# One PSUM pool for attention and the last layer, and a fixed order for TensorE's steps in a two-layer decoder trunk

## The chip, the cores and the metric

The kernel runs on one core of a Trainium2 chip. The metric is the time of one execution in microseconds (us) on the device; where several runs are compared, their median. The engines are called as in the profile: PE is TensorE (matmuls; PEld its weight loads), DVE is VectorE, ACT is ScalarE, POOL is GpSimd, SP is SyncE, which here issues DMAs. PSUM is the buffer that matmuls write to. It has eight banks, of 128 partitions by 512 fp32 numbers each.

## The reference, cut to what matters

512 tokens of width 1024, with 16 learned meta tokens ahead of them (528 positions), go through two layers and a final norm:

```python
h = concatenate([meta, x])                               # 528 x 1024
for i in range(2):
    a = rmsnorm(h, norm_mix[i])
    h = h + (pool_mixer(a, ...) if i == 0 else sb_mixer(a, w_qkv, w_o))
    n = rmsnorm(h, norm_ffn[i])
    h = h + (silu(n @ w_gate[i]) * (n @ w_up[i])) @ w_down[i]      # 1024 -> 2816 -> 1024
return rmsnorm(h, final_norm)[16:]

def sb_mixer(h, w_qkv, w_o):                             # 16 heads of 64
    q, k, v = (h @ w_qkv) split into heads
    z = q k^T / 8                                        # mask: key < query
    log_keep = where(mask, log_sigmoid(-z), 0)
    later = reverse_cumsum(log_keep) - log_keep
    a = where(mask, exp(log_sigmoid(z) + later), 0)
    return (a @ v) @ w_o
```

All of it is fp32.

## The kernel before

**Products.** Each fp32 product is made of three products of halves: weight and activation are split into a high part (a cast by ACT) and a low part (a subtraction by DVE), and `mm3` (L104) issues high x high, high x low and low x high into one PSUM tile. `wsplit` (L84) makes the halves of a weight block of 128 x 512; its raw block comes by DMA from SP's queue. In names, `...h` and `...l` are the halves.

**Stages.** Layer 0's pool mixer and feed-forward network (FFN) take the first 402 us, stick-breaking attention runs to about 685 us, layer 1's FFN and the final norm to the end.

**Attention** goes over eight pairs of heads. `proj` (L512) projects q, k and v of a pair in five steps of eight `mm3` each, into tiles `pj`; the first of all, `pj0_00`, is followed by the norm's product `abp` (ones x sums of squares, `norm_bcast` L167), whose result scales every projection. `Scores.group` (L572) makes the scores z of both heads in three groups, 832, 0 and 416, with a sigmoid of z (`sg`) and of -z (`kp`) by ACT behind each. DVE then runs, head by head, a reverse scan over `kp` (L594) and a product with `sg` (L596). `turned` (L603) transposes `sg` on PE (tiles `t1`, `t2`; `am` is a small strip that ACT copies for the last transpose), ACT and DVE split the result (`a1..`, `a2..`, and four small `a0` steps), and `attend` multiplies it with v into `po`. `wo` gives steps of the output projection, `pw{p0}_{c}`: product of the pairs from p0 on, added to the residual chunk `h{c}` by DVE (L673). The main loop interleaves: while pair p's weights are made, PE works on the projections of pair p+2, or, when none are left, on `wo` steps: w[0:4] (`pw2_0` to `pw2_3`) between pairs 6 and 7, w[4:6] behind the first transposes of pair 7.

**FFN of layer 1.** 22 blocks of 128 hidden columns. Blocks 0 to 3 are plain (`plain` L356: gate and up, tiles `pp`, operands `f1uh`, `f1ul`); inside block 0's up product the norm's product `fb1p` is made, from which DVE builds the scale `fb1` and, under `operands`, the normalized operands of the other blocks. Blocks 4 to 21 use Strassen's scheme (`strassen` L405): seven products instead of eight, in three PSUM accumulators pa, pb and pc: product 0 and 3 in pa, 1, 4 and 6 in pb, 2 and 5 in pc. The halves `m1`, `m6`, `m5` and `m67` are copied out by ACT (`keep`, L425) before the next product is accumulated onto pa, pb, pc and pb. Six ROUNDS of blocks each end in a down projection by tokens (`down_n` L323, tiles `pd`): 128 tokens x 512 columns (e = 0 or 1), added to `hn` by DVE. A round's down products are spread among the blocks of the next round. The last round's come at the end, by tokens t, each followed by `square` and `store` of `final` (L739): sums of squares by ACT, the root, a scale by ACT for the first 512 columns and by DVE for the other 512, two DMAs.

**PSUM.** Each stage opens a pool of its own (`phase` L66, `ps` L71): `ps1` with six tiles "w" and two "d" for layer 0's FFN, `ps2` with four "one" and two "two" (two banks each) for attention, `ps3` again with six "w" and two "d" for layer 1's FFN. A new pool's tiles wait until the old pool's banks are free.

**Order.** The engines execute their queues in order. A scheduler of the framework sets those orders when the program is built; `tc.issue_after(x)` makes it put what follows behind x. It also tracks, tile by tile, who must wait for whom. `begin` (L679) orders the scores' groups 0 and 1 behind the steps in `before`, and group 2 behind the steps in `between`.

Of the kernel before, what the change touches and what calls it, by code (L numbers as in the profile page):

```python
# [52 lines left out]
def trunk(ctx: ExitStack, tc: tile.TileContext, x, meta, x_t, gain, pool_w, w_qkv, w_o, w_gate, w_up, w_down,  # L53
# [49 lines left out]

    def mm3(outs, wh, wl, xh, xl, start, stop, more=False):  # L104

        for i, (w, xx) in enumerate(((wh, xh), (wh, xl), (wl, xh))):
            for o, sl in outs:
                last = nc.tensor.matmul(o, lhsT=w, rhs=xx[:, sl], start=start and i == 0, stop=stop and i == 2,  # L108
                                        skip_group_check=more)
# [164 lines left out]
    def ffn(layer, gcol, norm, after):  # L274
# [48 lines left out]
        def down_n(r, t, e, hid, w, tag="d", sl=slice(0, 512)):  # L323
# [8 lines left out]
            for j, (wh, wl) in enumerate(zip(*w)):  # L332
                for i, (x_, w_) in enumerate(((0, wh), (1, wh), (0, wl))):
                    nc.tensor.matmul(pd, lhsT=hid[j][x_][:, ts], rhs=w_[:, sl], start=r > 0 and i + j == 0,  # L334
                                     stop=j == len(hid) - 1 and i == 2, skip_group_check=r == 0)
# [3 lines left out]
            else:  # L339
                nc.vector.tensor_tensor(out=hv, in0=pd, in1=hv, op=ALU.add)  # L340
# [473 lines left out]
```

## Time and profile before

| what | value |
|---|---|
| runs | 1045.97, 1046.10, 1046.62 us; median 1046.1 |
| profiled execution | 1047.39 us, its span 1045.6 us, mean granted clock 0.991 |
| PE busy | 1017.1 us, 97% of the span |
| DVE busy | 846.4 us, 81% |
| ACT busy | 550.8 us, 53% |
| DMA | 95.7 MB, 92 GB/s on average |
| last matmul starts | 1037.36 us |

The span is what the profiler saw from the first to the last instruction; the execution's own time is 1.8 us longer. A PE that is busy is not always at its peak, since the ends of matmuls are modelled and the clock can be lower; the view of windows has the granted clock by stretch. In the view of groups and in the timeline a line reads: engine, line, operation, output <- inputs, and in brackets the idle time before it with what ended it. Names there leave out the numbers of layer, pair and buffer, so `pw` is `pw2_1` or any other.

### The profile page before, as it was taken

Reading aid. Unit: us, or ns where it says so; the run is one execution under the profiler, and the core shown is the slowest. Engines: PE = TensorE matmul, PEld = TensorE weight load, DVE = VectorE, ACT = ScalarE, POOL = GpSimd, SP = SyncE. Lnnn points to the kernel's source line nnn. Section 1 sums busy time; section 2 is a strip of 40 time slices with the busy share of each in tenths; the row PEclk is TensorE's granted clock in tenths of the full one; section 3 lists DMA queues with packets and bytes.
Section 4 is the critical chain, followed back from the end, with each engine's and each line's share of the span. In section 5 each row is a group of like instructions: output and inputs, shape, how many; then the busy total and the mean of one; then the engine's idle time right before and its main releaser. Section 6 shows DMA issues by size and latency. Waiting matters only on the chain.

```text
span 1045.6 us, 18479 instructions
## 1 busy us (share of the span) xinstructions
PE 1017.1 (97%) x7278; PEld 943.5 (90%) x7278; DVE 846.4 (81%) x1511; ACT 550.8 (53%) x1115; POOL 6.2 (1%) x16
## 2 busy tenths in 40 slices
PE   8999999999999999999999998999999999999996
PEld 6999999999999998988888886878999999999985
DVE  7999987888787777778888987779888777788755
ACT  7555544445545455455555455555655544445534
POOL 1000000000000010000000000000000000000000
PEclk9999999999999999999999998999999999999998
DMA  9222333333323332211111212122233323233302
GB/s 349 70 83 71 122 101 102 102 100 102 102 82 102 101 122 87 76 41 61 41 51 32 76 46 81 64 89 70 81 112 112 100 90 99 97 114 109 120 23 81
DMA packets 43112, 95.72 MB, mean 92 GB/s; under 512 B 3329, under 2 KB 20097, under 8 KB 43025
## 3 DMA queue, kind: packets, MB, share of 16 engines
q1 hardware_dynamic: 42272, 93.40, 27.2%
q8 instruction: 57, 0.93, 0.4%
q10 hardware_dynamic: 752, 1.14, 0.3%
q14 instruction: 31, 0.25, 0.1%
HBM read 92.43 MB, written 2.10 MB: 90 GB/s over the span
## 4 chain that ended last, share of the span: by engine, by line
PE 84%; DVE 11%; issue 2%; ACT 1%; DMA 1%; SPq 0%; ACTq 0%; DVEq 0%
PE pb L108 15%; PE pd L108 12%; PE pd L334 12%; PE pa L108 10%; PE pc L108 10%; PE pp L108 9%; PE pj L108 9%; DVE kp L594 2%; PE pw L108 2%; PE z L580 2%; DVE a L632 1%; PE t L607 1%; DVE sg L596 1%; PE mix L108 1%; DVE h L673 1%
## 5 line engine op out<-in xcount | busy, mean ns | idle before, releaser
L307 DVE TENSOR_TENSOR h<-pd,h 128x264 f32<-128x264 f32 x96 | 40.9, 427 | 14.9 <-PE pd L108 14.9
L594 DVE TENSOR_TENSOR_SCAN kp<-kp,estrip 128x1344 f32<-128x1344 f32 x16 | 47.3, 2954 | 3.8 <-ACT kp L589 3.4
L94 ACT CAST ws_3h<-rgate 128x512 fp32r<-128x512 f32 x36 | 22.4, 621 | 53.0 <-PE pb L108 47.8
L94 ACT CAST ws_5h<-s 128x512 fp32r<-128x512 f32 x36 | 22.4, 622 | 45.7 <-PE pb L108 33.3
L446 DVE TENSOR_TENSOR u<-pb,m 128x264 f32<-128x264 f32 (+1 forms) x36 | 15.4, 427 | 35.6 <-PE pb L108 35.5
L94 ACT CAST ws_4h<-s 128x512 fp32r<-128x512 f32 x36 | 22.4, 621 | 41.5 <-PE pa L108 24.4
L108 PE MATMUL pa<-xh,ws_0l 128*128 128x264 f32 (+1 forms) x144 | 40.9, 284 | 0.1
L108 PE MATMUL pc<-xh,ws_2h 128*128 128x264 f32 (+1 forms) x144 | 40.7, 282 | 0.3 <-ACT ws_2h L94 0.3
L108 PE MATMUL pa<-xh,ws_0h 128*128 128x264 f32 (+1 forms) x144 | 40.8, 283 | 0.0
L108 PE MATMUL pb<-xh,ws_1h 128*128 128x264 f32 (+1 forms) x144 | 40.8, 283 | 0.0
L108 PE MATMUL pb<-xh,ws_6l 128*128 128x264 f32 (+1 forms) x144 | 40.7, 283 | 0.0
L108 PE MATMUL pc<-xh,ws_2l 128*128 128x264 f32 (+1 forms) x144 | 40.7, 283 | 0.0
L108 PE MATMUL pb<-xl,ws_1h 128*128 128x264 f32 (+1 forms) x144 | 40.7, 283 | 0.0
L108 PE MATMUL pa<-xl,ws_3h 128*128 128x264 f32 (+1 forms) x144 | 40.7, 283 | 0.0
L108 PE MATMUL pb<-xh,ws_4l 128*128 128x264 f32 (+1 forms) x144 | 40.7, 283 | 0.0
L108 PE MATMUL pa<-xh,ws_3h 128*128 128x264 f32 (+1 forms) x144 | 40.7, 283 | 0.0
L108 PE MATMUL pb<-xh,ws_1l 128*128 128x264 f32 (+1 forms) x144 | 40.7, 283 | 0.0
L108 PE MATMUL pb<-xl,ws_4h 128*128 128x264 f32 (+1 forms) x144 | 40.7, 283 | 0.0
L108 PE MATMUL pc<-xl,ws_5h 128*128 128x264 f32 (+1 forms) x144 | 40.7, 282 | 0.0
L108 PE MATMUL pb<-xl,ws_6h 128*128 128x264 f32 (+1 forms) x144 | 40.7, 282 | 0.0
L108 PE MATMUL pc<-xh,ws_5h 128*128 128x264 f32 (+1 forms) x144 | 40.6, 282 | 0.0
L108 PE MATMUL pa<-xl,ws_0h 128*128 128x264 f32 (+1 forms) x144 | 40.6, 282 | 0.0
(1207 smaller groups left out, 4103.9 us busy)
## 6 DMA issues: line engine op xcount, KB each, us to landing
rgate<-in_ffn_w_gate_dram SPq DMA_DIRECT2D x44, 512.0 KB, 3.5
rup<-in_ffn_w_up_dram SPq DMA_DIRECT2D x44, 512.0 KB, 3.5
rd<-in_ffn_w_down_dram SPq DMA_DIRECT2D x42, 512.0 KB, 3.6
rq<-in_sb_w_qkv_dram SPq DMA_DIRECT2D x8, 512.0 KB, 3.4
rk<-in_sb_w_qkv_dram SPq DMA_DIRECT2D x8, 512.0 KB, 3.5
rv<-in_sb_w_qkv_dram SPq DMA_DIRECT2D x8, 512.0 KB, 3.5
rwo<-in_sb_w_o_dram SPq DMA_DIRECT2D x8, 384.0 KB, 3.0
h<-in_x_t_dram SPq DMA_DIRECT2D x8, 264.0 KB, 6.8
```

The costliest lines, as they stand in the source:

```text
L94: nc.scalar.copy(hi, v[:, j:j + w])
L108: last = nc.tensor.matmul(o, lhsT=w, rhs=xx[:, sl], start=start and i == 0, stop=stop and i == 2, skip_group_check=more)
L307: nc.vector.tensor_tensor(out=hv, in0=pd, in1=hv, op=ALU.add)
L334: nc.tensor.matmul(pd, lhsT=hid[j][x_][:, ts], rhs=w_[:, sl], start=r > 0 and i + j == 0, stop=j == len(hid) - 1 and i == 2, skip_group_ch ...
L446: tt(out=u[:, a], in0=pb, in1=m1, op=ALU.add)
L580: nc.tensor.matmul(tz[:, hd, c:c + k1 - k0], lhsT=qq[hs, i * P:(i + 1) * P], rhs=kk[hs, k0:k1], start=j == 0 and c == 0, stop=False, skip_ ...
L594: nc.vector.tensor_tensor_scan(kp[:, hd, ::-1], kp[:, hd, ::-1], estrip[:, ::-1], 1.0, op0=ALU.mult, op1=ALU.max)
L596: return nc.vector.tensor_tensor(out=sg[:, hd, 0:STRIP - 1], in0=sg[:, hd, 0:STRIP - 1], in1=kp[:, hd, 1:STRIP], op=ALU.mult).ins
L607: nc.tensor.transpose(o, sg[:, c0:c0 + n], ident)
L632: nc.vector.scalar_tensor_tensor(a0[r, i], f32(a0h[r]), lo_rows[r], p2[r, 256:384], op0=ALU.mult, op1=ALU.add)
L673: nc.vector.tensor_tensor(out=hT[c][:, TOK], in0=pj, in1=hT[c][:, TOK], op=ALU.add)
```

## The change

Five edits, on one diff:

- **One PSUM pool.** `ps2` now has two tiles "c", two "d" and two "two" (eight banks), and serves attention and layer 1's FFN; `ps3` is gone. "one" takes "c" and "d" in turn. `ps_pair` gives a plain block's two tiles (one two-bank tile, every third time two "c"), `ps_three` a Strassen block's three: pa and pb are the two banks of one tile "two", pc is a "c".
- **The norm's product** `abp` is issued inside the first projection, behind its fifth `mm3` group (k == FB) instead of behind the eighth.
- **`queued`** chains attention's PE steps, so that each is issued behind the one written before it.
- **LATE = 2**: in the last round, the last two down steps of the round before (r = 4, e = 1, t = 2 and 3) are held back and issued behind the last Strassen product (`prods_end`).
- **The last round's down products** are chained token by token; their e = 1 tiles have the tag "c"; the last token's scales and stores are cut into two pieces of 256 columns, with four DMAs instead of two.

```diff
-    def ps(name, tag, banks=1):
+        if tag == "one" and "c" in psum["bufs"]:
+            psum["turn"] = psum.get("turn", 0) + 1
+            tag = "cd"[psum["turn"] % 2]
...
+    def ps_pair(name):
+        if "w" in psum["bufs"]:
+            return [ps(f"{name}{j}", "w") for j in range(2)]
+        psum["pairs"] = psum.get("pairs", 0) + 1
+        if psum["pairs"] % 3 == 0:
+            return [ps(f"{name}{j}", "c") for j in range(2)]
+        pt = ps(name, "two", 2)
+        return [pt[:, 0], pt[:, 1]]
+    def ps_three(name):
+        if "w" in psum["bufs"]:
+            return [ps(f"{name}{j}", "w") for j in range(3)]
+        pt = ps(name, "two", 2)
+        return [pt[:, 0], pt[:, 1], ps(f"{name}c", "c")]
...
-                pa, pb, pc = [ps(f"p{i}{f}", "w")[:, :n] for i in "abc"]
+                pa, pb, pc = [t[:, :n] for t in ps_three(f"p{f}")]
...
                             for t in range(4):
-                                down_n(r - 1, t, e, prev, w)
+                                rest.append(lambda r=r, t=t, e=e, prev=prev, w=w: down_n(r - 1, t, e, prev, w))
+                            while len(rest) > (LATE if r == len(ROUNDS) - 1 else 0):
+                                rest.pop(0)()
...
+            for st in rest:
+                with tc.issue_after(prods_end[0]):
+                    st()
             square, store = after()
...
-                    down_n(r, t, e, prev, ws[e], "dw"[e], sl)
+                    with tc.issue_after(mark) if mark else nullcontext():
+                        mark = down_n(r, t, e, prev, ws[e], "dc"[e], sl)
...
-    with tc.tile_pool(name="att", bufs=1) as ap, phase("ps2", one=4, two=2):
+    ctx.enter_context(phase("ps2", c=2, d=2, two=2))
+    with tc.tile_pool(name="att", bufs=1) as ap:
...
-                if not rbs:
-                    rb = norm_bcast([acc], "ab", "one")
+                    if not rbs and k == FB:
+                        with tc.issue_after(last):
+                            rbs.append(norm_bcast([acc], "ab", "one"))
+                        mark = last_bcast[0]
...
+        pos = []
+        def queue():
+            return tc.issue_after(pos[0]) if pos else nullcontext()
+        def queued(*steps):
+            for st in steps:
+                with queue():
+                    pos[:] = [st()]
...
-            mark = None
-            for st in before:
-                mark = st()
-            with tc.issue_after(mark) if mark else nullcontext():
-                sc.group(0)
-                mark = sc.group(1)
-            for st in between:
-                with tc.issue_after(mark):
-                    mark = st()
-            with tc.issue_after(mark):
-                sc.group(2)
+            queued(*before, lambda: (sc.group(0), sc.group(1))[1], *between, lambda: sc.group(2))
...
+            w = 512 if t < 3 else 256
+            cuts = [slice(o, o + w) for o in range(0, 512, w)]
+            for sl in cuts:
+                nc.scalar.activation(hvs[0][:, sl], box[0][:, 16 + sl.start:16 + sl.stop], AF.Copy, scale=r)
...
-    ctx.enter_context(phase("ps3", w=6, d=2))
     ffn(1, 24, norms[1], final)
```

Three places show how the orders move. The number behind a name's last underscore is only a buffer's.

**PE between pairs 6 and 7.** Rows are PE's; pw2_1 to pw2_3 are `wo` steps, z7_416 the last scores of pair 7. Before:

```order
L108 MATMUL pw2_1_8108<-os4h_7521,wo2_1l0_8105 128x512
L108 MATMUL pw2_2_8146<-os2h_6813,wo2_2h0_8142 128x512
...
L108 MATMUL pw2_2_8146<-os4h_7521,wo2_2l0_8143 128x512
L108 MATMUL pw2_3_8161<-os2h_6813,wo2_3h0_8157 128x512
...
L108 MATMUL pw2_3_8161<-os2h_6813,wo2_3l0_8158 128x512
L580 MATMUL z7_416_8119<-qk7_1h_7770,qk7_0h_7832 128x400 x2
L580 MATMUL z7_416_8119<-qk7_1h_7770,qk7_0h_7832 128x16 x2
...
L586 MATMUL z7_416_8119<-masks_63 128x128
L108 MATMUL pw2_3_8161<-os3h_7141,wo2_3h0_8157 128x512
```

and in the change:

```order
L132 MATMUL pw2_1_8108<-os4h_7521,wo2_1l0_8105 128x512
L625 MATMUL z7_416_8119<-qk7_1h_7770,qk7_0h_7832 128x400 x2
L625 MATMUL z7_416_8119<-qk7_1h_7770,qk7_0h_7832 128x16 x2
...
L631 MATMUL z7_416_8119<-masks_63 128x128
L132 MATMUL pw2_2_8146<-os2h_6813,wo2_2h0_8142 128x512
```

The scores z7_416 move ahead of twelve products: all nine of pw2_2 and the first three of pw2_3. DVE's queue, which works for the same pair, in the change, from the scan of head 0 to the four a0 of head 0:

```order
L639 SCALAR_TENSOR_TENSOR kp7_8056<-kp7_8056,estrip_5463 128x1344
L730 TENSOR_TENSOR h2_68<-pw2_2_8146,h2_68 128x512
L121 TENSOR_TENSOR wo5_2l0_8394<-rwo5_2_8391,wo5_2h0_8393 128x384
L641 TENSOR_TENSOR sg7_8055<-sg7_8055,kp7_8056 128x1343
L639 SCALAR_TENSOR_TENSOR kp7_8056<-kp7_8056,estrip_5463 128x1344
L730 TENSOR_TENSOR h3_69<-pw2_3_8161,h3_69 128x512
L121 TENSOR_TENSOR wo5_3l0_8416<-rwo5_2_8391,wo5_3h0_8415 128x384
L706 TENSOR_TENSOR of6_7905<-po61_8172,sh61_8182 64x512
L641 TENSOR_TENSOR sg7_8055<-sg7_8055,kp7_8056 128x1343
L686 TENSOR_TENSOR a170l_8208<-t170_8194,a170h_8207 128x1024
L686 TENSOR_TENSOR a270l_8210<-t270_8195,a270h_8209 128x256
L689 SCALAR_TENSOR_TENSOR a0_5471<-a0h70_8211,consts_61,t270_8195 32x128 x4
```

Before, h2 and wo5_2l stood ahead of the first scan, h3 and wo5_3l ahead of the first product with sg, and os6l, h4 and wo5_4l ahead of a270l; now h2 stands behind the first scan, h3 behind the second, and the three behind the a0 steps.

**PE at the start of layer 1's FFN.** pw5_6 and pw5_7 are the last `wo` steps, pp0, pp1 and pp20 the gate products of blocks 0, 1 and 2. Before:

```order
L108 MATMUL pw5_5_8465<-os7h_8342,wo5_5l0_8462 128x512
L108 MATMUL pw5_6_8489<-os5h_7901,wo5_6h0_8485 128x512
...
L108 MATMUL pw5_7_8511<-os7h_8342,wo5_7l0_8508 128x512
L108 MATMUL pp0_8574<-f1uh0_8363,wgate0h0_8553 128x512
L108 MATMUL pp0_8574<-f1ul0_8364,wgate0h0_8553 128x512
```

and in the change:

```order
L132 MATMUL pw5_5_8465<-os7h_8342,wo5_5l0_8462 128x512
L132 MATMUL pp0_8570<-f1uh0_8363,wgate0h0_8549 128x512
L132 MATMUL pw5_6_8489<-os5h_7901,wo5_6h0_8485 128x512
...
L132 MATMUL pw5_7_8511<-os7h_8342,wo5_7l0_8508 128x512
L132 MATMUL pp0_8570<-f1ul0_8364,wgate0h0_8549 128x512
L132 MATMUL pp0_8570<-f1uh0_8363,wgate0l0_8550 128x512
L132 MATMUL pp0_8570<-f1uh1_8384,wgate0h0_8549 128x512
L132 MATMUL pp1_8766<-f1uh0_8363,wgate1h0_8745 128x512
L132 MATMUL pp1_8766<-f1ul0_8364,wgate1h0_8745 128x512
```

The first row of pp0 has moved ahead of pw5_6's nine and pw5_7's nine, and the first two of pp1 among pp0's; two of pp20 follow further on, all ahead of fb1p.

**The last Strassen block, 21.** m1, m6, m5 and m67 are the copies of its PSUM halves, ws21 its weights, wd1_18 those of the last down projection. ACT before:

```order
L425 COPY m1_12328<-pa21_12313 128x256
L94 CAST ws21_5h0_12305<-s3_12280 128x512
L94 CAST ws21_6h0_12309<-rup1_21_12275 128x512
L94 CAST wd1_18_0h0_12430<-rd1_18_0_12428 128x512
L94 CAST wd1_18_0h1_12434<-rd1_18_0_12428 128x512
L94 CAST wd1_20_0h0_12440<-rd1_20_0_12438 128x512
L425 COPY m6_12342<-pb21_12314 128x256
L94 CAST wd1_20_0h1_12444<-rd1_20_0_12438 128x512
L425 COPY m5_12356<-pc21_12315 128x256
```

and in the change:

```order
L116 CAST ws21_5h0_12253<-s3_12228 128x512
L116 CAST ws21_6h0_12257<-rup1_21_12223 128x512
L378 CAST hh20_12141<-u20_12132 128x512
L454 COPY m6_12289<-p21_12261 128x256
L454 COPY m5_12303<-p21c_12262 128x256
L116 CAST wd1_18_0h0_12405<-rd1_18_0_12403 128x512
L116 CAST wd1_18_0h1_12409<-rd1_18_0_12403 128x512
L454 COPY m67_12329<-p21_12261 128x256
```

hh20 has moved from ahead of m1 to right ahead of m6, and wd1_18's casts behind m6 and m5. PE in the change at the end of product 1 (ws21_1) and the beginning of product 3 (ws21_3):

```order
L132 MATMUL p21_12261<-xh1_8534,ws21_1h0_12237 128x256
L132 MATMUL p21_12261<-xl1_8541,ws21_1h0_12237 128x256
L132 MATMUL p21_12261<-xh1_8534,ws21_1l0_12238 128x256
L132 MATMUL p21_12261<-xh3_8536,ws21_3h0_12245 128x256
L132 MATMUL p21_12261<-xl3_8543,ws21_3h0_12245 128x256
```

Product 3 follows product 1 at once; before, product 2 lay between them, and a piece of the last down projection between products 3 and 4.

SP's and POOL's queues keep their order; only the last token's two stores have become four.

More of the change, by code (lines that the diff above doesn't have):

```diff
@@ L31 @@
 PLAIN = 4
+LATE = 2
 FB = 4
@@ L102, in wsplit @@
         return his, los
+    last_mm = []
     def mm3(outs, wh, wl, xh, xl, start, stop, more=False):
@@ L109, in mm3 @@
                                         skip_group_check=more)
+        last_mm[:] = [last.ins]
         return last.ins
@@ L333, in down_n @@
                 for i, (x_, w_) in enumerate(((0, wh), (1, wh), (0, wl))):
-                    nc.tensor.matmul(pd, lhsT=hid[j][x_][:, ts], rhs=w_[:, sl], start=r > 0 and i + j == 0,
-                                     stop=j == len(hid) - 1 and i == 2, skip_group_check=r == 0)
+                    last = nc.tensor.matmul(pd, lhsT=hid[j][x_][:, ts], rhs=w_[:, sl], start=r > 0 and i + j == 0,
+                                            stop=j == len(hid) - 1 and i == 2, skip_group_check=r == 0)
             hv = hn[4 * e + t][:, sl]
@@ L340, in down_n @@
                 nc.vector.tensor_tensor(out=hv, in0=pd, in1=hv, op=ALU.add)
+            return last.ins
         with tc.tile_pool(name=f"ffn{layer}", bufs=1) as fp:
@@ L362, in plain @@
                 prods = []
+                pair = None
                 for i, (dst, (wh, wl)) in enumerate(zip((g, u), parts)):
-                    pts = [ps(f"pp{f}", "w")[:, :sl.stop - sl.start] for sl in pieces]
+                    if full or not i:
+                        pair = ps_pair(f"pp{f}")
+                    pts = [t[:, :sl.stop - sl.start] for t, sl in zip(pair if full else pair[i:], pieces)]
                     prods.append((dst, pts))
@@ L453, in ffn @@
             fst = []
+            rest = []
             prev = None
@@ L524, in half @@
                 pj = ps(f"pj{p}_{i}{hf}", "one")[:, :n]
+                mark = None
                 for k in range(KC):
-                    last = mm3([(pj, sl)], wh[k], wl[k], uh[k], ul[k], k == 0, k == KC - 1)
-                if not rbs:
-                    rb = norm_bcast([acc], "ab", "one")
+                    with tc.issue_after(mark) if mark else nullcontext():
+                        last = mm3([(pj, sl)], wh[k], wl[k], uh[k], ul[k], k == 0, k == KC - 1)
+                    if not rbs and k == FB:
+                        with tc.issue_after(last):
+                            rbs.append(norm_bcast([acc], "ab", "one"))
+                        mark = last_bcast[0]
+                if len(rbs) == 1:
+                    rb = rbs.pop()
                     r8 = blk("r8")
@@ L699, in trunk @@
         sg = begin(0, got, [], steps[3:4])
-        steps[4]()
+        queued(steps[4])
         values()
         nxt, steps, values = proj(1)
-        for st in steps[:3]:
-            st()
+        queued(*steps[:3])
         early, w = wo(0, 2), wo(2, 5)
@@ L709, in trunk @@
             w0 = turned(p, 0, sg[:, 0])
-            for st in steps[3:] if p + 1 < NP else w[4:6]:
-                st()
+            queued(*(steps[3:] if p + 1 < NP else w[4:6]))
             if p + 1 < NP:
                 values()
-            attend(p, 0, w0, v, of)
+            queued(lambda: attend(p, 0, w0, v, of))
             w1 = turned(p, 1, sg[:, 1])
@@ L725, in trunk @@
                 sg = begin(p + 1, got, fill[0], fill[1])
-            for st in fill[2]:
-                st()
-            attend(p, 1, w1, v, of)
+            queued(*fill[2], lambda: attend(p, 1, w1, v, of))
             if p in (4, 5):
```

31 lines of the change are left out of this document (18 added, 13 removed).

## The prediction

> **What bounds it now.** I read the page first, then TensorE's waits, then granted clock and busy time by stretch, then the chain of waits where TensorE stands still.
>
> ```profile
> span 1045.6 us, 18479 instructions
> ...
> PE 1017.1 (97%) x7278; PEld 943.5 (90%) x7278; DVE 846.4 (81%) x1511; ACT 550.8 (53%) x1115; POOL 6.2 (1%) x16
> ```
>
> TensorE (PE) bounds the span. The change takes no matmul away, so only PE's idle time, its slow clock and the stretch behind its last product can shrink. The waits from 402 us on:
>
> ```profile
> PE t L607 <- DVE sg L596: 3.6, 1, 3.6
> PE pp L108 <- DVE h L673: 2.3, 1, 2.3
> PE z L580 <- ACT qk_1h L540: 1.6, 1, 1.6
> ```
>
> The longest three are single waits in three places, and the change rearranges all three. The rest are 0.2 to 0.5 us each, inside pairs 0 to 5 of attention, where the order stays.
>
> ```profile
> 402.00:640.00 238.00, 229.19 (x1637) 202.84 (x1638) 191.71 (x274) 130.16 (x261) 0.00 (x0) 1.00 0.17 56
> ...
> 645.00:650.00 5.00, 1.41 (x9) 1.12 (x8) 5.00 (x5) 1.16 (x5) 0.00 (x0) 0.78 0.23 65
> 650.00:655.00 5.00, 5.00 (x18) 4.28 (x17) 4.94 (x4) 1.63 (x2) 0.00 (x0) 0.54 0.10 40
> 685.00:690.00 5.00, 5.00 (x16) 3.90 (x16) 4.85 (x8) 2.64 (x5) 0.00 (x0) 0.66 0.00 0
> 698.00:745.00 47.00, 47.00 (x233) 39.01 (x231) 46.51 (x95) 25.77 (x55) 0.00 (x0) 1.00 0.24 79
> 752.00:1014.00 262.00, 262.00 (x1833) 244.42 (x1832) 205.48 (x367) 135.19 (x277) 0.00 (x0) 1.00 0.31 99
> ```
>
> Columns: stretch and length; busy time of PE, weight loads, DVE, ACT and POOL; granted clock; DMA share; GB/s. From 402 to 640 waits of up to 1.6 us leave the clock at 1.00. After the 3.6 us wait it is 0.78 and 0.54: with a half clock as the low state, 5 x 0.22/0.5 + 5 x 0.46/0.5 = 6.8 us of it. After the 2.3 us wait it is 3.4 us. From 752 to 1014 PE never idles, so nothing is to be gained there; from 698 to 745 VectorE (DVE) is busy 46.5 of 47 us.
>
> **Pair 6 to 7 (the 3.6 us).**
>
> ```profile
> 636.70 4.95 PE pw L108 x21
> 641.65 0.98 PE z L580 x12
> ...
> 643.78 2.96 DVE kp L594
> 646.74 0.58 DVE h L673
> 647.32 0.46 DVE wo_3l L99
> 647.78 1.48 DVE sg L596
> 649.26 0.14 issue
> 649.40 2.37 PE t L607 x10
> ...
> 660.13 0.93 PE pw L108 x4
> ```
>
> One product of 512 columns takes 4.95/21 = 0.236 us. Of those 21, nine finish pw2_1 and twelve more stand ahead of z7_416, whose sigmoid feeds the scan for the transposes t. The new order puts z7_416 right behind pw2_1: 12 x 0.236 = 2.8 us earlier. ACT's sigmoid and DVE's scan move with it, the scan to 640.95. Behind it the changed DVE order is h2, wo_2l, sg of head 0, the scan of head 1, h3, wo_3l, of, sg of head 1, a170l, a270l, four a.
>
> ```profile
> 652.15 0.68 DVE L649 TENSOR_TENSOR of<-po,sh 64x512 f32<-64x512 f32 x1
> 652.87 1.56 DVE L596 TENSOR_TENSOR sg<-sg,kp 128x1343 f32<-128x1343 f32 x1
> 654.34 1.22 DVE L629 TENSOR_TENSOR a170l<-t,a170h 128x1024 fp32r<-128x1024 f32 x1
> ...
> 657.47 1.45 DVE L632 SCALAR_TENSOR_TENSOR a<-a0h,consts,t 32x128 fp32r<-32x128 f32 x4
> ```
>
> With these lengths, a little overlapped as there: sg of head 0 ends at 646.5, PE's t starts at 646.6 instead of 649.4 (it has come to the end of po61 at 645.6, so 1.0 us idle), head 1's scan ends at 649.35, h3 at 650.0, of at 651.1, sg at 652.65, a170l at 653.8, the last a at 655.5. PE, at full clock, finishes the transposes at 647.8 and pw2_4 and pw2_5 (18 x 0.236) at 652.2; po70 then waits 1.4 us for a170l and 0.6 for the last a. Then come eleven transposes of head 1, which before were hidden in po70's gaps (1.2 us), so pw2_6 starts near 657.1 instead of 660.0. **2.9 us** gained, not 3.6 plus a slow clock: DVE becomes what is late next. The new waits are shorter than the 1.6 us that left the clock full, so I take no slow clock. Ends: 1.4 if one half-clock stretch of 3.4 us remains, and 3.6 + 6.8 x 0.455 = 6.7 if DVE never held PE (at half clock a product costs 0.43, so 45% of such time is lost).
>
> [...]
>
> **Start of the last layer (the 2.3 us).**
>
> ```profile
> 684.87 10.86 PE pp L108 x39
> 695.73 0.89 PE fb1p L175 x4
> ...
> 687.23 0.76 DVE L155 SCALAR_TENSOR_TENSOR f1ul<-h,gains,f1uh 128x528 fp32r<-128x528 f32 x1
> ...
> 698.26 0.71 DVE L138 TENSOR_TENSOR fb1t<-fb1r 128x528 f32<-128x528 f32 x1 [5.68 <-ACT fb1r L137]
> ```
>
> The first pp waits for the last h, the last reader of the attention's PSUM. With one pool it stands ahead of pw5_6, and four products of blocks 1 and 2 fill in. The tightest operand is the last f1ul: ready at 688.0 today, perhaps 0.6 later with an ACT cast now ahead of it, and used 26 products behind the last pw, at 682.4 + 6.1 = 688.5. I take no wait. PE gains 2.3 us of idle and 10.86 - 39 x 0.236 = 1.7 of slow clock, 4.0 together. fb1p comes 43 products behind the last pw: 682.4 + 10.1 = 692.5 instead of 695.7, so DVE's saturated stretch begins only 3.2 us earlier. At its end, in the first Strassen block, nine products of 256 columns (1.06 us) now come later, and the casts before pd and ws5_0 have less in front of them: I book 0.6 lost there. **3.4 us**; ends 2.4 and 4.0.
>
> **The norm's product (the 1.6 us).**
>
> ```profile
> 415.50 0.43 DVE L532 TENSOR_TENSOR qf<-pj,abr 128x264 f32<-128x264 f32 x1
> ...
> 415.96 0.63 ACT L540 CAST qk_1h<-qf 128x528 fp32r<-128x528 f32 x1 [0.41 <-DVE qf L532]
> ...
> 416.64 0.74 PE L580 MATMUL z<-qk_1h,qk_0h 64*128 64x512 f32 x6 [1.63 <-ACT qk_1h L540]
> ```
>
> abp, whose result scales the projections, moves up by nine products of 512 columns, 2.1 us, and DVE's scalings with it. But qk_1h also needs the projection pj_11, and that ends where PE's idle time begins, at 416.64 - 1.63 = 415.0; scaling (0.43) and cast (0.63), with 0.1 of hand-over, put z at 416.2. **0.45 us**; ends 0 and 1.6.
>
> **PSUM in the Strassen blocks.** Seven products go to pa, pb and pc. pa and pb now lie in one tile, so a product for one waits until the copy of the other's earlier half is made.
>
> ```profile
> L425 ACT COPY m<-pb 128x256 f32<-128x256 f32 x35 | 12.8, 366 | 0.0
> L94 ACT CAST wd_0h<-rd 128x512 fp32r<-128x512 f32 x20 | 12.1, 621 | 7.6 <-PE pb L108 4.0 <-PE pc L108 2.1 <-PE pa L108 0.9
> ```
>
> A copy needs the product's end (0.28), perhaps a cast ahead of it (0.62), and 0.37: 1.3 us. In the new order 14 or more products of 0.118 (1.65 us) lie between, in all blocks but the last, so nothing is lost. Only block 6's first product finds twelve (1.4 us) in front of the product's end, a cast, a subtraction as long as DVE's of (0.68) and u4's half-width read of the tile (0.42 like the add below): 0.28 + 0.62 + 0.68 + 0.42 = 2.0, some 0.15 of it overlapped: **-0.45**. Ends 0 and -5.4 (0.3 us in each of 18 blocks).
>
> **Two steps held back.** They run behind block 21's last product, where their 24 products (5.7 us) stand in for PE while ACT and DVE finish u21; but PE waits for nothing there today, since products of the last round lie in front. Now block 21 has no filler: its product 3 follows product 1 at once and waits for copy m6. In ACT's new order two casts stand ahead of that copy, the first released one product before the last: 0.28 + 0.62 + 0.62 + 0.37 = 1.9, less two products of 0.12 that run anyway. **-1.6**; ends 0 and -2.2 (one more cast ahead of copy m67). Behind the wait stand only block 21's other products and the two held steps. The last round by tokens adds no wait to PE: each token has 24 products (5.7 us), and an add of half a row takes 0.42 (below).
>
> **The end.**
>
> ```profile
> 1037.24 0.28 PE L334 MATMUL pd<-wd_1h,hl 128*128 128x256 f32 x1
> 1037.36 0.28 PE L334 MATMUL pd<-wd_1l,hh 128*128 128x256 f32 x1
> ...
> 1037.67 0.42 DVE L340 TENSOR_TENSOR hn<-pd,hn 128x256 f32<-128x256 f32 x1
> ...
> 1038.60 0.40 ACT L751 ACTIVATE fsq<-hn 128x256 f32<-128x256 f32 x1
> ...
> 1039.90 0.75 DVE L762 SCALAR_TENSOR_TENSOR hn<-hn,fss,gb 128x512 f32<-128x512 f32 x1
> ...
> 1041.15 0.72 ACT L761 ACTIVATE hn<-fss 128x512 f32<-128x512 f32 x1 [0.47 <-DVE fss L141]
> 1041.54 0.34 ACTq L764 DMA_DIRECT2D out_dram<-hn  x1
> ```
>
> The span runs 8.0 us past PE's end (1037.64). Tokens 2 and 3 finish together: token 3's last square waits behind two others until 1038.60, and its scale until 1041.15, behind token 2's scale on DVE (1039.90). In the change token 2 is done 5.7 us earlier. The last square follows its add at 1038.1; from a square's end to the scale 2.15 us pass today, less the 0.75: the scale starts at 1038.1 + 0.4 + 1.4 = 1039.9, 1.25 earlier. Two half scales cost 0.08 more, and ACT's second, new DMA issue 0.34, though each of the four carries half. SP has the other new one; else SP's and POOL's queues keep their order. **+1.0**; ends 0.4 and 1.9.
>
> **Sum.** 0.45 + 2.9 + 3.4 - 0.45 - 1.6 + 1.0 = 5.7 us. The profiled execution took 1047.39 us (1045.6 in the span, 1.8 around it), 1.3 above the runs' median of 1046.1. So 1041.7 for such an execution and **1040.4** for the median.
>
> **Rivals.** *A: copies stall every Strassen block.* One more cast ahead of two copies per block costs 2 x (0.62 - 0.35 of slack) = 0.54, in 18 blocks 9.7 us: 1050.1, slower. It decides from 5.7/18 = 0.32 us a block on. For it: casts wait for the same products as the copies. Against: ACT works 135 of 262 us, and most copies have 22 to 47 products in front. *B: part comes back.* A half-clock stretch of 3.4 us stays at pair 7 (1.55 us), or DVE, which starts only 3.2 us earlier, holds PE before 745 and leaves 2.4 of the 3.4 there: 1041.4, 1042.0, or 1043.0 with both. For it: 46.5 of 47 us; against: PE waits for nothing there today. [...] *C: more is gained.* Block 21's casts find their operands later than the copy, the last layer's start keeps 4.0 and the end gives 1.9: 5.7 + 1.6 + 0.6 + 0.9 = 8.8, so 1037.3. *D: the change does not do what it says:* the first pp still waits. The order has it ahead of pw5_6 with another PSUM slot, so 2 in 100: 1046.1 - 5.7 + 3.4 = 1043.8.
>
> **Chances.** Forecast 0.62, A 0.10, B 0.15, C 0.11, D 0.02. The likeliest alone spans 1038.5 to 1042; with B and most of C, 1037.0 to 1044.5. A measurement of this kernel tells 0.2% (2.1 us) from no change: faster takes the forecast, C, D and B nearly whole, 0.87; same 0.06; slower, most of A, 0.07.
>
> **What would show it.** Step by step: t waits about 1 us at pair 7 and po70 about 2, at clock 1.00; pp L108 no longer waits for h, and 685 to 690 has clock 1.00; z's wait for qk_1h falls to 1.2; a wait of pa for an ACT copy of 1.6 us in the last block, and none in the others; the last product is followed by 7.0 instead of 8.0 us. Wrong if PE waits for L454's copies in many blocks, or the clock falls near 650 again.

## The result, and the profile after

| | median of the runs | range | ratio to before, 95% interval |
|---|---|---|---|
| before | 1046.03 us (4 runs) | 1045.94 to 1046.62 | |
| the change | 1040.87 us (4 runs) | 1039.50 to 1042.71 | 0.9948 [0.9932, 0.9964] |

The change is 0.5% faster. The profiled execution took 1040.96 us (1047.39 before). Its page begins:

```profile
span 1039.2 us, 18506 instructions
...
PE 1014.0 (98%) x7278; PEld 940.2 (90%) x7278; DVE 846.9 (81%) x1512; ACT 550.3 (53%) x1116; POOL 6.2 (1%) x16
```

The span is 6.4 us shorter. PE is busy for 3.0 us less with the same 7278 matmuls, mostly time at half clock that is gone. The rest went from its idle time (2.0 us) and from the stretch behind its last product (1.4 us). PE's waits after the change (released by; us in total, times, longest), those that replace the three of before and those that are new:

```profile
PE p L132 <- ACT m L454: 1.4, 1, 1.4
...
PE po L703 <- DVE a170l L686: 1.3, 1, 1.3
PE z L625 <- ACT qk_1h L585: 1.2, 1, 1.2
...
PE t L663 <- DVE sg L641: 0.8, 1, 0.8
...
PE pd L359 <- ACT wd_1h L116: 0.2, 1, 0.2
PE p L132 <- DVE u L476: 0.2, 1, 0.2
```

No first `pp` of the last layer waits for `h` any more. `t` waits 0.8 us instead of 3.6, and `po70` behind it 1.3. The copy `m` holds PE once, 1.4 us long, in one block. The same stretches as in the prediction, by busy time and granted clock (the third column from the right):

```profile
645.00:650.00 5.00, 4.17 (x25) 3.28 (x24) 4.97 (x5) 2.62 (x8) 0.00 (x0) 1.00 0.00 0
650.00:655.00 5.00, 3.34 (x17) 2.38 (x15) 4.89 (x9) 2.02 (x7) 0.00 (x0) 1.00 0.33 105
...
685.00:690.00 5.00, 5.00 (x23) 4.13 (x23) 4.26 (x7) 1.61 (x3) 0.00 (x0) 1.00 0.16 35
...
698.00:745.00 47.00, 46.62 (x247) 38.96 (x246) 45.94 (x96) 26.56 (x60) 0.00 (x0) 1.00 0.25 79
```

The clock is full at 650 and at 685 us, where 6.8 and 3.4 us of half clock were. From 698 to 745 us VectorE is as busy as before, and PE now idles 0.4 us. Three moments of PE's timeline of before, and the same three of after, give the gain place by place: the first product of `pw2_6`, the first down product behind block 2, and the last product of all (1037.36 before, shown in the prediction).

```profile
659.97 0.39 PE L108 MATMUL pw<-os2h,wo_6h 128*128 128x512 f32 x1
...
720.81 0.60 PE L328 MATMUL pd<-consts,h 128*128 128x128 f32 x4
```

```profile
646.06 1.28 PE L663 MATMUL t<-consts,sg 128*128 128x128 f32 x10 [0.83 <-DVE sg L641]
...
653.32 0.50 PE L703 MATMUL po<-a170l,vv 128*128 128x512 f32 x1 [1.32 <-DVE a170l L686]
...
654.98 0.51 PE L703 MATMUL po<-a,vv 128*128 128x512 f32 x1 [0.34 <-DVE a L689]
...
656.45 0.48 PE L132 MATMUL pw<-os2h,wo_6h 128*128 128x512 f32 x1
...
713.28 0.60 PE L353 MATMUL pd<-consts,h 128*128 128x128 f32 x4
...
1032.30 0.28 PE L359 MATMUL pd<-wd_1l,hh 128*128 128x256 f32 x1
```

The scores z start at 416.06 instead of 416.64: 0.6 us. At `pw2_6` the lead is 3.5 us, so pairs 6 to 7 gave 2.9. At the end of block 2 it is 7.5, so the start of the last layer gave 4.0. At the last product it is 5.1: 2.5 us were lost again on the way. Compared at the same number of columns multiplied, the lead falls by 1.0 us between 735 and 760 us, gains 0.2 in small pieces up to 990 us, and falls by 1.65 in block 21. Block 21 in ACT's timeline:

```profile
997.33 0.62 ACT L116 CAST ws_6h<-rup 128x512 fp32r<-128x512 f32 x1 [0.74 <-PE p L132]
997.86 0.61 ACT L378 CAST hh<-u 128x512 fp32r<-128x512 f32 x1
998.38 0.37 ACT L454 COPY m<-p 128x256 f32<-128x256 f32 x1
```

The copy stands behind two casts, and product 3 starts at 998.80, when it is done. PE in the same place:

```profile
997.13 0.28 PE L132 MATMUL p<-xh,ws_1l 128*128 128x256 f32 x1
998.80 0.39 PE L132 MATMUL p<-xh,ws_3h 128*128 128x256 f32 x1 [1.38 <-ACT m L454]
999.02 0.28 PE L132 MATMUL p<-xl,ws_3h 128*128 128x256 f32 x1
```

This wait cost more than its idle time. Products of 256 columns start 0.118 us apart when nothing waits, though each is recorded for 0.28. Here the next starts 1.67 us later, and the one behind it 0.22: 1.65 us are lost, not 1.4. Counted the same way, the 1.0 us between 735 and 760 us lie at short waits, against before: 0.2 at `wd_1h`, 0.25 at the first products of block 5 and 0.5 at u4. The last steps on ACT:

```profile
1033.08 0.42 ACT L795 ACTIVATE fsq<-hn 128x256 f32<-128x256 f32 x1 [0.46 <-DVE hn L365]
...
1034.69 0.91 ACT L808 ACTIVATE hn<-fss 128x256 f32<-128x256 f32 x2 [0.68 <-DVE fss L166]
```

The last square no longer waits behind others; from the end of the last product (1032.58) to the end of the span 6.6 us pass, 8.0 before.

### The profile page after: what moved, and what is told of

Read it like the earlier page. It is cut to its first block, busy times and chain, and to the rows that moved or that the text cites. A ratio compares the mean times of both kernels' runs of the same rounds, so it can differ in the third digit from the quotient of the medians.

```text
span 1039.2 us, 18506 instructions
## 1 busy us (share of the span) xinstructions
PE 1014.0 (98%) x7278; PEld 940.2 (90%) x7278; DVE 846.9 (81%) x1512; ACT 550.3 (53%) x1116; POOL 6.2 (1%) x16
## 5 line engine op out<-in xcount | busy, mean ns | idle before, releaser
L454 ACT COPY m<-p 128x264 f32<-128x264 f32 (+1 forms) x126 | 46.1, 371 | 0.0
L132 PE MATMUL p<-xh,ws_3h 128*128 128x264 f32 (+1 forms) x144 | 40.7, 283 | 1.4 <-ACT m L454 1.4
L132 PE MATMUL p<-xh,ws_0h 128*128 128x264 f32 (+1 forms) x144 | 41.0, 285 | 0.4 <-DVE u L476 0.2
L132 PE MATMUL p<-xh,ws_0l 128*128 128x264 f32 (+1 forms) x144 | 40.9, 284 | 0.0
L132 PE MATMUL p<-xh,ws_6l 128*128 128x264 f32 (+1 forms) x144 | 40.8, 283 | 0.0
L132 PE MATMUL p<-xh,ws_4l 128*128 128x264 f32 (+1 forms) x144 | 40.8, 283 | 0.0
L132 PE MATMUL p<-xh,ws_1h 128*128 128x264 f32 (+1 forms) x144 | 40.8, 283 | 0.0
L132 PE MATMUL p<-xl,ws_1h 128*128 128x264 f32 (+1 forms) x144 | 40.7, 283 | 0.0
L132 PE MATMUL p<-xl,ws_3h 128*128 128x264 f32 (+1 forms) x144 | 40.7, 283 | 0.0
L132 PE MATMUL p<-xh,ws_1l 128*128 128x264 f32 (+1 forms) x144 | 40.7, 282 | 0.0
```

The source lines that it names most:

```text
L454: nc.scalar.copy(t, o)
```

## The experiments

Times are medians; the interval is that of the ratio to before. One thing has to be known to read them: times of one and the same kernel fall into groups 0.7 to 1.9 us apart, and the mean granted clock goes with the group. Ten runs of the change in two batches gave 1039.3 to 1039.5 us (twice, clock 0.999), 1040.8 to 1041.0 (four times, 0.997) and 1042.7 (four times, 0.995); 23 runs of before in one batch gave 1045.1 to 1045.5 (7 times, 0.994), 1045.9 to 1046.7 (11 times, 0.993) and 1047.3 to 1047.9 (5 times, 0.991). What the groups are came out of e1 to e3. Small effects are therefore read within a group, or from the trace.

**e1: the chain alone, on the kernel before.**

```diff
 # before, with only:
+    queued(*before, lambda: (sc.group(0), sc.group(1))[1], *between, lambda: sc.group(2))
+    with queue():          # around the transposes; steps and attend through queued() too
```

> The kernel before with one edit of the change: attention's TensorE steps chained one behind the other; both PSUM pools, the place of the norm's product, the Strassen blocks and the tail are as before. My theory: the 2.9 us at pairs 6 to 7 come from this chain alone, because z7_416 is issued 12 products earlier. So t waits 0.8 us for sg (3.6 before), po70 waits about 1.7 us for a170l and a, the clock stays 1.00 from 645 to 655 us, and the wait of pp for the last h (2.3 us) and its 3.4 us of half clock remain: 1046.0 - 2.9 = 1043.1 us. Rival: the PSUM slots of the shared pool let z7_416 go earlier; then t still waits 3.6 us here, and the time is 1046.0. Second rival: the gain is eaten by a longer wait of pp for h; then it is 1046.0 with t at 0.8 us and pp at 5 us.

Measured: 1044.50 us (12 runs, 1043.05 to 1046.23), ratio 0.9982 [0.9974, 0.9991]. The waits:

```profile
PE pp L132 <- DVE h L728: 2.3, 1, 2.3
...
PE po L701 <- DVE a170l L684: 1.3, 1, 1.3
...
PE t L661 <- DVE sg L639: 0.8, 1, 0.8
```

The waits are those expected (the 1.3 us of po70 are those for a170l alone), and the profiled execution (1044.43) lies 2.96 us below that of before (1047.39). So the chain makes the gain at pair 7, not the pool, and it isn't eaten at `pp`. By medians the gain is only 1.6 us: 5 of the 12 runs were at 1043.1, 5 at 1044.4 to 1044.9, and 2 at 1046.1 and 1046.2.

**e2: the two pools put back into the change.**

```diff
-    ctx.enter_context(phase("ps2", c=2, d=2, two=2))
+    with ... phase("ps2", one=4, two=2):
 ...
+    ctx.enter_context(phase("ps3", w=6, d=2))
```

> The changed kernel with the two PSUM pools of before put back (attention four and two, the last layer six and two; pa, pb and pc in tiles of their own); all else as changed, the two held-back steps too. My theory: the start of the last layer loses what it gained (pp waits 2.3 us for h again, 3.4 us of half clock: 4.1 us), while block 6's wait (0.2) and block 21's wait for the copy (1.4) go away, since product 3 then waits for copy m1 alone, and the wait of pd for wd_1h (0.25) goes too: 1040.9 + 4.1 - 1.9 = 1043.1 us. Rival on block 21: its wait comes from the missing filler alone, whatever the tiles; then 1.4 us stay and it is 1044.5. Rival on the start: another operand (f1ul) holds pp anyway, and then nothing is lost there: 1039.0.

Measured: 1041.34 us (5 runs, 1041.32 to 1042.46), ratio 0.9957 [0.9945, 0.9969]. `pp` waits 2.3 us for `h` again, and no product waits for a copy: both as expected, so in block 21, which has no filler, sharing one tile is what makes PE wait. But the time is 1.8 us below the expectation, since the 2.3 us brought no half clock. It is somewhere else in this execution. Stretches of 3.41 us, laid so that their bounds fall on the clock's changes:

```profile
650.15:653.56 3.41, 1.78 (x10) 1.09 (x8) 3.34 (x7) 1.06 (x6) 0.00 (x0) 1.00 0.29 117
653.56:656.97 3.41, 3.38 (x14) 3.10 (x15) 3.40 (x6) 1.43 (x2) 0.00 (x0) 0.50 0.00 0
677.45:680.86 3.41, 1.91 (x9) 1.21 (x7) 3.41 (x6) 3.11 (x6) 0.00 (x0) 1.00 0.14 55
680.86:684.27 3.41, 2.57 (x11) 2.15 (x12) 3.41 (x7) 3.00 (x6) 0.00 (x0) 1.00 0.00 0
```

The waits of 1.3 and 0.3 us for a170l and a, which left the clock full in the change's profile, here stand in one such stretch (PE busy 1.78 of 3.41 us), and the next has half clock. The wait of 2.3 us is split by a bound into 1.5 and 0.8 us (busy 1.91 and 2.57), and the clock stays full. So the length of a wait alone doesn't tell whether half clock follows. Stretches laid in this way are called steps of the grid below; their bounds lie at other places of the program in other executions (647.81 and 651.22 us in the change's profile, 650.15 and 653.56 here). From these rows I took as a working assumption that the idle time in one step decides: that is the theory of the grid in the expectations.

**e3: no step held back.**

```diff
-LATE = 2
+LATE = 0
```

> The changed kernel with no steps held back (LATE = 0): the 24 products of the two steps go back among the Strassen blocks. My theory: block 21's product 3 no longer waits for the copy (1.4 us gained), but nothing now stands between its last product and the first token's products; in the profile after, the low half of u21 was ready 4.1 us after the last product, and the first token has nine products of other blocks (2.1 us) in front of it, so a new wait of 1.0 to 1.9 us for hh or hl appears there: together 1040.4 to 1041.4 us, no difference that can be told from the change. Rival: PE waits for nothing there, as in the kernel before, and the 1.4 us are kept: 1039.5.

Measured: 1044.68 us (11 runs, 1043.90 to 1045.59), ratio 0.9985 [0.9977, 0.9994]: 3.8 us slower than the change, where I had expected none. One row of its waits, and three steps of the grid:

```profile
PE pd L359 <- ACT hh L378: 3.1, 1, 3.1
```

```profile
1008.27:1011.68 3.41, 1.19 (x10) 0.98 (x9) 2.90 (x6) 1.28 (x4) 0.00 (x0) 1.00 0.00 0
1011.68:1015.09 3.41, 2.53 (x5) 1.78 (x6) 1.42 (x3) 0.62 (x1) 0.00 (x0) 0.50 0.00 0
1015.09:1018.50 3.41, 3.41 (x9) 2.64 (x8) 0.99 (x3) 0.72 (x2) 0.00 (x0) 0.50 0.00 0
```

The copy's wait is gone, but it is filled with the first token's nine ready products: eight of them stand ahead of block 21's product 3 and one ahead of its last product. They can't fill twice. Behind the last product nothing is left but the three that need u21, so PE waits 3.1 us for its cast, and 6.8 us of half clock follow. The wait of 1.0 to 1.9 us that I had expected was right in kind, and its size assumed that the nine products stayed where they were. The two held-back steps are worth 3.8 us.

**e4: tiles of its own in block 21 alone.**

```diff
+                if f == 21 and not full:
+                    tiles = ps(f"p{f}", "two", 2)[:, 0], ps(f"p{f}b", "c"), ps(f"p{f}c", "d")
```

> The changed kernel with one difference: in block 21 alone pa, pb and pc lie in three tiles of their own, so product 3 (into pa) waits for the copy of pa, and not for that of pb. The two steps stay held back. My theory: the wait of 1.4 us in block 21 goes to 0 and nothing else moves: 1040.9 - 1.4 = 1039.5 us. Rival: the wait is one for the missing filler, and product 3 or 4 waits as long for another copy: 1040.9 us.

Measured: 1039.57 us (5 runs, 1038.22 to 1039.73), ratio 0.9934 [0.9922, 0.9946]. The row `p <- ACT m` is gone from its waits and the others are unchanged. Its group with clock 0.996 to 0.997 lies at 1039.3 to 1039.7, 1.3 below that of the change; expected were 1.4. In the trace its lead on the change grows by 1.6 us at block 21. Together with e2 this shows the cause: the copy of pb's half, on which pa's product 3 has to wait only because both lie in one tile.

**e5: VectorE's chain at pair 7 made shorter.**

```diff
         for c, st in enumerate(wo(5, NP)):
-            st()
+            with tc.issue_after(held[0] if c < 4 else held[1]) if c > 1 else nullcontext():
+                st()
```

> The changed kernel with six subtractions of VectorE moved: the low halves of the weights of pw5_2 to pw5_5 (wo_2l to wo_5l) are held behind the last small a step of pair 7's second head, or behind the add of pw2_7; TensorE's order is the same. In the profile after, wo_2l stands between the scan and the product of head 0 and wo_3l between the scan of head 1 and a170l, 0.5 us each. My theory: VectorE's chain sets the time at pair 7, so t waits 0.3 instead of 0.8 us for sg, the chain to the last a is 1.0 us shorter, and PE behind it starts 1.0 us earlier: 1040.9 - 1.0 = 1039.9 us. Rival: ACT's casts or PSUM slots set it; then the waits of t (0.8) and po70 (1.3 and 0.3) stay, 1040.9. Second rival: the four subtractions, done late, are late for pw5_2, and PE waits there for what was gained.

Measured: 1039.31 us (5 runs, 1038.86 to 1040.51), ratio 0.9933 [0.9920, 0.9945]. PE's timeline:

```profile
645.72 1.28 PE L663 MATMUL t<-consts,sg 128*128 128x128 f32 x10 [0.35 <-DVE sg L641]
...
652.52 0.51 PE L703 MATMUL po<-a170l,vv 128*128 128x512 f32 x1 [0.85 <-DVE a170l L686]
...
655.64 0.49 PE L132 MATMUL pw<-os2h,wo_6h 128*128 128x512 f32 x1
```

`pw2_6` starts 0.8 us earlier than in the change (0.9 counted from z, which started 0.1 later here), and nothing waits later for the subtractions held back: 1.0 was expected. VectorE is what pair 7 waits for. Execution by execution the gain reads as 0.4 us only (1038.9 to 1039.1 against 1039.3 to 1039.5 at clock 0.999); the span of this profile is 0.9 us shorter, but 2.2 us lie around it and not 1.8.

**e6: e4 and e5 together.**

> The two together: VectorE's subtractions held behind pair 7 as in e5, and block 21 with tiles of its own as in e4 (which took the wait of 1.4 us away). Both theories: two waits in different places add up, 1.0 + 1.35 us below the changed kernel: 1038.5 us, the fastest of all; if e5 gains nothing, 1039.5.

Measured: 1038.70 us (5 runs, 1037.10 to 1038.83), ratio 0.9921 [0.9909, 0.9933]. The two gains add up: in the trace 0.9 us at pair 7 and 1.6 at block 21, and at clock 0.997 the times (1038.6 to 1038.8) lie 2.1 us below the change's.

**e7 and e8: a wait made longer on purpose.**

```diff
                 nc.vector.tensor_tensor(out=f[:, sl], in0=pj, in1=rbs[i][:, sl], op=ALU.mult)
+                for _ in range(4 if p == 0 and i == 1 and hf == 1 else 0):      # e8: 8
+                    nc.vector.tensor_scalar(f[:, sl], f[:, sl], 1.0, None, op0=ALU.mult)
```

> The changed kernel with four multiplications by 1.0 on VectorE (128 x 264, about 0.25 us each by the 0.43 us of one of 128 x 528) between the last scaling of the first pair and the cast that z waits for, so that the wait of z for qk_1h grows from 1.2 to about 2.2 us. [...] Time: 1040.9 + 1.0 and, with the slow step, + 1.5 more: 1041.9 or 1043.4. Rival: a wait of a fixed length (about 2.3 us, as the prediction took it) is the limit; then the clock stays 1.00 behind z in every execution, and the time is 1041.9.

> The same with eight multiplications: z waits about 3.1 us. Theory of the grid: one step or the next always holds 1.5 us or more of it, so nearly every execution has half clock behind z: 1040.9 + 1.9 + 1.5 = 1044.3 us. [...]

Measured: e7 1045.79 us (10 runs, 1043.69 to 1047.48), e8 1046.77 us (10 runs, 1045.23 to 1048.14). A multiplication took 0.3 us and not 0.25, and a subtraction of 0.68 us (`wv1l`) ran between the first and the second, so the waits became 3.0 and 4.3 us. Both are longer than I wanted, both times lie above all that were expected, and by length alone the waits don't tell the grid from a fixed limit of 2.3 us. Only one execution of each was profiled, so how often half clock follows such a wait isn't shown. What the two runs add are steps of known idle time, e7's at z (2.34 us) and e8's at pair 7 (1.57):

```profile
415.63:419.04 3.41, 1.07 (x8) 0.78 (x10) 2.25 (x6) 1.75 (x2) 0.00 (x0) 1.00 0.47 144
419.04:422.45 3.41, 3.41 (x22) 2.41 (x19) 0.00 (x0) 2.58 (x4) 0.00 (x0) 0.50 0.05 14
```

```profile
657.72:661.13 3.41, 1.84 (x10) 1.51 (x11) 3.33 (x8) 0.99 (x5) 0.00 (x0) 1.00 0.12 49
661.13:664.54 3.41, 3.41 (x15) 3.12 (x14) 3.41 (x7) 2.04 (x4) 0.00 (x0) 0.50 0.12 11
```

In e8 the unchanged waits of pair 7 (1.2 and 0.35 us) fell into one step (PE busy 1.84 of 3.41 us) and were followed by half clock, as in e2 (1.78).

**e9: the change once more.** The kernel is unchanged.

> The changed kernel itself once more, for its spread. Theory of the grid: its times fall on steps about 1.5 us apart, by how many stretches of half clock an execution has (0 at 1039.5, one at 1040.9, two at 1042.5 us), and a higher mean granted clock goes with a lower time. Rival: the spread has another cause; then time and clock don't go together.

Measured: 1041.79 us (6 runs, 1039.30 to 1042.73), ratio 0.9958 [0.9946, 0.9970]; these are the groups told above, and time and clock go together. The medians of the two batches, 1040.87 and 1041.79, differ by how many runs fell into which group.

**e10: the norm's product moved back.**

```diff
-                    if not rbs and k == FB:
+                    if not rbs and k == KC - 1:
```

> The changed kernel with the norm's product abp behind the whole first projection again. My theory: z waits 1.6 instead of 1.2 us for qk_1h, and the kernel is 0.45 to 0.6 us slower: 1041.4 us. Rival: qk_1h doesn't depend on it in time (the cast waits for pj_11 alone), and nothing changes: 1040.9.

Measured: 1041.71 us (5 runs, 1041.46 to 1043.21), ratio 0.9965 [0.9953, 0.9977]; at clock 0.996 to 0.997 0.7 us above the change. PE's timeline:

```profile
412.15 0.39 PE L132 MATMUL pj<-anuh,wk0h 128*128 128x264 f32 x1 [0.19 <-DVE abt L165]
...
416.81 0.73 PE L625 MATMUL z<-qk_1h,qk_0h 64*128 64x512 f32 x6 [1.44 <-ACT qk_1h L585]
```

z starts 0.7 us later than in e9's profile (416.12). Only part of that is the wait for qk_1h. `pj_11` now waits 0.2 us for the slot of abp and starts at 412.15; in the kernel before, with abp in the same place and two pools, it started at 411.82 without a wait. So the edit also takes away a wait that the shared pool would have brought.

**e11: the last token's scales and stores in one piece.**

```diff
-            w = 512 if t < 3 else 256
+            w = 512
```

> The changed kernel with the last token's scales and stores in one piece each, as before; the token chain stays. My theory: of the 1.3 us that the stretch behind TensorE's last product got shorter (8.0 to 6.6), 1.1 come from the chain, since token 2's squares and scale are out of the way, and 0.2 from the cut: 6.8 us behind the last product, 1041.1 us. Rival: the cut gives most of it (shorter scales, and four smaller transfers that land sooner); then the stretch is 7.5 us or more.

Measured: 1039.76 us (6 runs, 1039.46 to 1042.74), ratio 0.9949 [0.9937, 0.9962]; its runs at clock 0.999 (1039.5 to 1040.0) lie on the change's (1039.3 and 1039.5). The last scale in its profile:

```profile
1033.04 0.72 ACT L808 ACTIVATE hn<-fss 128x512 f32<-128x512 f32 x1 [0.68 <-DVE fss L166]
```

PE's last product ended at 1030.94 and the span at 1037.38: 6.4 us, less than the 6.6 with the cut. Two half scales take 0.91 us and a whole one 0.72, and the transfers give nothing back. The whole gain at the end comes from the chain by tokens; the cut costs 0.2 us. These 0.2 us are read from the traces (6.6 us in nine of the ten profiles with the cut, 7.2 in e7; 6.4 in e11 and e12); the times don't tell them.

**e12: e6 and e11, with PE's idle time at 17 to 20 us filled.**

```diff
                     nc.tensor.matmul(pp, lhsT=ah[i][:, cs], rhs=rhs, start=j == 0, stop=False)
+                    for _ in range(5 if hf == 1 and c == 0 and j > 0 else 0):
+                        nc.tensor.matmul(pp, lhsT=warm[:, 0:P], rhs=warm[:, :HALF], start=False, stop=False)
```

> The kernel of e6 (VectorE's subtractions held behind pair 7, block 21 with tiles of its own) with the last token's scales in one piece as in e11, and with ten products of zeros (128 x 264, 0.12 us each) added where TensorE waits in layer 0's pool mixer, five ahead of each of the two waits for al (0.93 and 0.69 us at 17 to 20 us). They add zero to the sums and need nothing that comes later. Theory of the grid: half clock at 20 us follows a grid step in which PE idled 1.62 us; with 1.1 us of it filled, no step behind the start holds 1.55 us of waits in attention or before, so no execution has half clock there, and all times lie close together near the fastest of e6 (1037.1): 1036.9 to 1037.5 us. Rival: half clock at 20 us has nothing to do with PE's idle time; then the times lie on two steps, 1037.1 and 1038.7, as in e6.

Measured: 1037.00 us (4 runs: 1036.76, 1036.99, 1037.02, 1038.49), ratio 0.9910 [0.9894, 0.9927]: the fastest kernel here. Two steps of before's grid in layer 0, then the same place in e12, and in e11, which has no products of zeros:

```profile
16.32:19.73 3.41, 1.80 (x11) 1.21 (x9) 2.81 (x4) 3.41 (x7) 0.00 (x0) 1.00 1.07 385
19.73:23.14 3.41, 3.40 (x16) 3.29 (x16) 3.41 (x9) 2.91 (x8) 0.00 (x0) 0.50 1.03 410
```

```profile
14.76:18.17 3.41, 3.19 (x26) 2.74 (x25) 2.58 (x7) 2.78 (x4) 0.00 (x0) 1.00 1.06 379
18.17:21.58 3.41, 3.15 (x21) 2.57 (x22) 3.41 (x8) 3.30 (x9) 0.00 (x0) 1.00 1.04 403
```

```profile
14.73:18.14 3.41, 2.48 (x21) 2.19 (x19) 2.58 (x6) 2.78 (x5) 0.00 (x0) 1.00 1.08 383
18.14:21.55 3.41, 2.71 (x18) 2.29 (x19) 3.41 (x8) 3.29 (x9) 0.00 (x0) 1.00 1.02 406
```

Half clock at 20 us stood in 9 of the 14 profiled executions: in those whose grid, like before's, put both waits (0.93 and 0.68 us there) into one step. In e2, e3, e4 and e11 a bound split them (at 18.14 us in e11's rows) and the clock stayed full. In e12's profile the bounds lie as in e11's, so the trace doesn't show that the products of zeros did anything. Three of four runs lie within 0.3 us; without the products, e11 had four of six in its fastest group. The fourth, 1.5 us above, missed the expectation; which step it lost isn't known, since it wasn't the profiled one. Whether filling idle time keeps the clock up stays open.

## Why the prediction was right, and where it was not

| step | predicted | measured |
|---|---|---|
| norm's product | +0.45 | +0.6 |
| pair 6 to 7 | +2.9 | +2.9 |
| start of the last layer, less what is lost at 735 to 760 (block 6 among it) | +3.4 - 0.45 | +4.0 - 1.0 |
| small pieces from 760 to 990 | 0 | +0.2 |
| block 21 | -1.6 | -1.65 |
| the end | +1.0 | +1.4 |
| sum, span of the profiled execution | 5.7 | 6.4 |

- **Norm's product.** z waits 1.2 us as forecast. e10 confirms the size (0.7) and adds a cause that I hadn't seen, the slot of abp.
- **Pair 6 to 7.** Right in size and in mechanism: t waits 0.8 (1.0 said), po70 1.3 and 0.3 (1.4 and 0.6), `pw2_6` starts at 656.45 (657.1 said, without the lead of the norm's product). e1 shows that the chain does it, e5 that VectorE is next.
- **Start of the last layer.** The first pp waits for nothing, 4.0 was said for PE and 4.0 came. What was booked as lost behind it, 0.6 and 0.45, was 0.45 (pd and block 5) and 0.5 (u4), once the waits are counted from start to start.
- **Block 21.** The casts ahead of the copy and the loss are as worked out, 1.65 for 1.6. I had taken the missing filler and the shared tile for one cause; it takes both. Tiles of their own take the wait away without a filler (e2, e4), and with products in front there is none on the shared tile either (eight of them in e3; so too in the other 17 blocks). And what I wrote of the held-back steps, that PE waits for nothing there today, left out that the new chain by tokens makes them necessary: without them e3 loses 3.8 us.
- **The end.** Mis-sized: the stretch is 6.6 us and not 7.0. I had charged the cut 0.08 us and another issue; it costs 0.2 (e11), and the chain gives 1.5 instead of 1.25.
- **The clock is the step that failed.** I took the waits of up to 1.6 us that left the clock full, and the one of 2.3 that didn't, for a limit by length. e2 has a wait of 2.3 us with full clock and one of 1.3 and 0.3 us with half clock. So neither the 1.7 us at `pp` nor the absence of slow clock at pair 7 is certain in an execution; both are likely.
- **From the profile to the median.** I carried the 1.3 us between before's profiled execution and its median over to the change. Before's profile has four steps of half clock (one at 20, two at 648, one at 685 us) and is of the slowest of its three groups, while the change's has one and lies at its median (1040.96 and 1040.87). So 1041.7 for the profile was 0.7 too much, 1040.4 for the median 0.5 too little: a sum too small and a shift too large, which partly made up for each other.

Of the rivals, A is refuted: copies hold PE in one block of 18. B's second part, VectorE holding PE before 745 us, didn't come beyond the 1.0 us of the table; its first, half clock at pair 7, isn't in this profile but is in e2's and e8's, so some of the change's runs at 1042.7 may have had it (none of them was profiled). C comes half true at the end (1.4 us, between the 1.0 of the forecast and its 1.9) and nowhere else. D is refuted.

## What to carry to other kernels

Look at whether a wait is one of the data or of a tile: pa's product waited for a copy of pb because the two banks were one tile and nothing stood in front, and a tile of its own in one block was worth as much as half of the pair-7 edit. Products that fill a wait can fill only one; before steps are reordered, count which wait each of them covers now (e3). And before a profile is compared with a median, count its steps of half clock: here before's profile had four and the change's one, at up to 1.5 us each.

## What the runs showed of the hardware

In before's profile the granted clock was 0.50 from 19.71 to 23.13, from 647.76 to 654.59 and from 685.31 to 688.72 us, so for 3.41, 6.83 and 3.41 us, and 1.00 between; from the end of one of these stretches to the start of the next 183 and 9 times 3.41 us passed. In the change's profile it was 0.50 once before the last product, from 19.75 to 23.17 us. Under half clock products of 512 columns started 0.43 us apart (before at 686 to 688 us), against 0.236 at full clock, and those of 264 columns 0.22 us apart (20 to 23 us), against 0.12. The first two groups of the change's times lie 1.45 us apart, and one such stretch has 3.41 x (1 - 0.236 / 0.43) = 1.5 us to lose, an estimate from the 0.43 and 0.236 for a stretch in which PE always has work.

In the rows of the experiments half clock followed full-clock steps in which PE was busy 1.07 (e7), 1.19 (e3), 1.78 (e2), 1.80 (before) and 1.84 us (e8) of 3.41. It didn't follow those with 1.91 (e2), 2.48 (e11) and 3.19 us (e12).

Busy or idle time doesn't sort all steps, though. In layer 0 of before and of the change a wait of 1.63 us, up to 40.02 us, fell whole into one step, and the clock stayed full behind it. And at the end of e5's kernel PE idled 1.89 us of a step, more than in three that were followed by half clock (1.57 in e8, 1.61 in before, 1.63 in e2), and the next step was still at full clock:

```profile
36.80:40.21 3.41, 1.78 (x15) 1.60 (x14) 3.41 (x8) 2.27 (x5) 0.00 (x0) 1.00 0.00 0
40.21:43.62 3.41, 3.41 (x29) 3.41 (x29) 3.41 (x6) 3.41 (x7) 0.00 (x0) 1.00 0.03 5
```

```profile
1030.20:1033.61 3.41, 1.52 (x13) 1.32 (x12) 2.08 (x10) 1.40 (x7) 0.00 (x0) 1.00 0.41 154
1033.61:1037.02 3.41, 0.00 (x0) 0.00 (x0) 1.00 (x3) 0.91 (x2) 0.00 (x0) 1.00 0.46 154
```

The first two rows are steps of before's grid. PE is as busy there (1.78 us) as in the step at 16.32 us (1.80), which was followed by half clock. The two differ in what PE ran: 15 products of 264 columns here against nine of 264 and two of 32 there. Busy time hides that, since a product that stands alone was recorded for 0.28 us or more (0.39 at 18.26 us), while dense ones started 0.12 us apart (at 37 us). No run sets idle time against the number of products, so what the clock goes by isn't shown.
